# A hybrid encoder layer in float32: weights of the gates and of two forget-attention groups split ahead and kept in DRAM, dq projections two blocks to a bank, loads reckoned longer

## The chip, the cores and the metric

The kernel runs on one core of a Trainium2 chip. The metric is the device time of one launch in microseconds, the median of three runs. The core has five engines with queues of their own: TensorE (matmuls, PE in the profile, its weight loads PEld), VectorE (DVE), ScalarE (ACT), GpSimd (POOL) and SyncE (SP), which here issues the DMA transfers in order.

## The reference

One layer over 1024 positions of width 1024, in float32: a gated feed-forward, a mixer of two attention branches, and a second gated feed-forward, each behind a modulated RMS norm.

```python
x = x + 0.5 * mod[:, 0, 2][:, None, :] * swiglu(modulate(x, ...), ffn1_w1, ffn1_w3, ffn1_w2)
h = modulate(x, norm_g[l, 1], mod[:, 1, 0], mod[:, 1, 1])
z = h @ w_in      # fq, fk, fv, ff | dq, dk, dv, iq, ik, iw | ga, gb
ya = fox_attention(rms_norm(fq), rms_norm(fk), fv, cumsum(log_sigmoid(ff + bias)))
yb = dsa_attention(rope(rms_norm(dq)), rope(rms_norm(dk)), dv, iq, ik, iw, top_k=256)
x = x + g2 * ((sigmoid(ga) * (ya @ w_br_fox) + sigmoid(gb) * (yb @ w_br_dsa)) @ w_out)
x = x + 0.5 * mod[:, 2, 2][:, None, :] * swiglu(modulate(x, ...), ffn2_w1, ffn2_w3, ffn2_w2)
```

For this change the projection `h @ w_in` matters: the gates `ga`, `gb` (2 x 1024 columns), the four forget groups (two heads' fq, fk, fv each, 384 columns) and the two dq groups (256 columns).

## The kernel before

**Split numbers.** A float32 product is made of three matmuls (`mm3`, L435): every operand is split into a high part `hi`, its value rounded to the matmul's own format by a ScalarE copy, and a low part `lo = src - hi` by a subtraction on VectorE or GpSimd. `mm3` adds hi x hi, hi x lo and lo x hi in a PSUM bank.

**The stages.** (1) First feed-forward, 0 to 688 us: its three products by a Strassen-like scheme of seven products over 11 pairs of blocks. `up_all` walks through 130 steps of one product (12 matmuls each); per step `steps` may hold extra calls, and `extra` makes the conditioning vectors beside it. `Down` makes the second half. Weights are split as they are used, VectorE making the low parts. (2) Statistics of the norm (`stats`), a first small projection (`first`, `norm_apply`), and the first three weight pieces of the first forget group (`k.early`), 688 to 723 us. (3) Two forget groups beside the index scores, 723 to 850 us. (4) The top-k stage, 850 to 1050 us: VectorE and ScalarE find the 256th score of each row, 32 bits one after the other (`topk`: VectorE counts for three row blocks, ScalarE by signs for the other three), while TensorE works through forget groups 2 and 3, dq groups 0 and 1 and the 16 gate blocks of the first 512 positions. (5) Attention, 1050 to 1400 us, with the 16 gate blocks of the other 512 positions and the masks between. (6) The output product and the second feed-forward, to 2229 us.

**Loading a weight in the mixer.** `load_w` takes a raw tile from the ring `k.w`, loads into it, takes a pair `wh`, `wl`, copies on ScalarE and subtracts on GpSimd (`k.lo_eng`). Each ring has raw tiles and pairs: one raw and three pairs at first, three raws and five pairs in stages 3 and 4 (`r5`), two and two in the attention (`r2`). `Ahead` keeps three pieces loaded before their use (one in the attention). The gate weights `w_g` are 16 pieces of 128 x 1024, used once per half of the positions, so each is loaded and split twice; forget weights are 4 pieces of 128 x 768 per group, dq weights 4 of 128 x 512.

**PSUM.** In the top-k stage `pq` holds eight banks: two tiles `p2` of two banks each, and four tiles `pj` of one. A wide group (`group`, forget 2 and 3, dq 0 and 1) keeps eight accumulators, one per block of 128 positions, over four weight pieces; `chain8` deals it four halves of `p2` and four `pj`. In the last of the four rounds `done` copies each finished accumulator out on ScalarE (tile `qkv`). The gates accumulate in `pj`.

**The order.** The order of all engines is written out by a planner (`Plan`): each call becomes a task, and `flush` places the tasks by list scheduling with estimated lengths, in the rank of the program order plus `behind`; a task may take a new buffer only within a window of ranks (200 in the first feed-forward, 600 later). The queues then run in just that order, each instruction waiting for its operands. A transfer is reckoned by these lines:

```python
self.wire = max(self.wire, s + 1.3) + t.bytes / 345e3
end = self.wire + 0.7
```

A GpSimd task and a VectorE task that both use only SBUF are placed one after the other (`self.port`). `t512` takes half-kilocolumn buffers from a common ring, 52 of them in the first feed-forward.

## Time and profile before

| | |
|---|---|
| median of 3 runs | 2230.95 us (2229.25 to 2231.05) |
| the profiled execution | 2230.78 us, its span 2229.0 us |
| busy: TensorE, VectorE, ScalarE, GpSimd | 97%, 74%, 51%, 11% of the span |
| TensorE in the chain that ended last | 82% |
| moved by DMA | 315.88 MB, 142 GB/s on average |
| granted clock of TensorE, mean | 0.994 |

Busy time of TensorE counts overlapped matmuls, so the better measure of a stretch is its number of matmuls and its idle time. Nearly every instruction has one line (L425, where the planner issues), so tiles tell which operation a row is: `bs`, `b` are feed-forward accumulators, `p` and `pj` the halves of `p2` and the single banks of the mixer, `qkv` a projection copied out of PSUM, `ir` the relu of an index score, `tk...` the top-k, `pr` and `mn` the attention's scores and their row minimum, `pth`, `ptl` transposed weights of the attention split in two, `wr`, `wh`, `wl` a weight raw, high and low.

### The profile page before, as it was taken

Reading aid. Unit: us, or ns where it says so; the run is one execution under the profiler, and the core shown is the slowest. Engines: PE = TensorE matmul, PEld = TensorE weight load, DVE = VectorE, ACT = ScalarE, POOL = GpSimd, SP = SyncE. Lnnn points to the kernel's source line nnn. Section 1 sums busy time; section 2 is a strip of 40 time slices with the busy share of each in tenths; the row PEclk is TensorE's granted clock in tenths of the full one; section 3 lists DMA queues with packets and bytes.
Section 4 is the critical chain, followed back from the end, with each engine's and each line's share of the span. In section 5 each row is a group of like instructions: output and inputs, shape, how many; then the busy total and the mean of one; then the engine's idle time right before and its main releaser. Section 6 shows DMA issues by size and latency. Waiting matters only on the chain.

```text
span 2229.0 us, 31185 instructions
## 1 busy us (share of the span) xinstructions
PE 2166.7 (97%) x10700; PEld 1782.9 (80%) x10700; DVE 1638.6 (74%) x3095; ACT 1145.2 (51%) x2105; POOL 252.0 (11%) x225
## 2 busy tenths in 40 slices
PE   7999999999999999989999998999999999999999
PEld 5877788887889899977777777777778888888887
DVE  7968776688684698888887677498865755558665
ACT  5634433444464566787777677244443333334443
POOL 0000000000010222223445343000000000000000
PEclk9999999999999999999999999999999999999999
DMA  9245543695421323235232212596224443258520
GB/s 333 95 149 178 173 152 109 213 351 195 125 89 57 109 78 130 96 123 161 90 120 88 72 39 81 202 354 189 66 81 132 137 130 103 96 207 287 166 76 38
DMA packets 186267, 315.88 MB, mean 142 GB/s; under 512 B 27238, under 2 KB 51814, under 8 KB 186108
## 3 DMA queue, kind: packets, MB, share of 16 engines
q1 hardware_dynamic: 186108, 313.89, 42.4%
q8 instruction: 84, 1.38, 0.3%
q14 instruction: 75, 0.61, 0.1%
HBM read 237.53 MB, written 76.28 MB: 141 GB/s over the span
## 4 chain that ended last, share of the span: by engine, by line
PE 82%; DVE 8%; ACT 5%; DMA 3%; issue 2%; SPq 0%; POOL 0%; DVEq 0%; ACTq 0%; POOLq 0%
PE bs L425 34%; PE b L425 28%; PE py L425 7%; PE pj L425 6%; PE p L425 5%; PE pt L425 2%; DVE qkv L425 1%; ACT tks L425 1%; DVE xc L425 1%; DMA mraw<-in_ada_w 1%; DMA wr<-in_w_f 1%; ACT pth L425 1%; ACT pr L425 1%; ACT wh L425 1%; DVE wl L425 1%
## 5 line engine op out<-in xcount | busy, mean ns | idle before, releaser
L425 PE MATMUL bs<-h,wh 128*128 128x512 f32 x1728 | 543.0, 395 | 1.6 <-ACT bs L425 1.3
L425 ACT ACTIVATE wh<-wr 128x512 fp32r<-128x512 f32 (+2 forms) x366 | 246.5, 679 | 451.7 <-PE bs L425 208.3
L425 PEld LDWEIGHTS bs<-h,wh 128*128 128x128 f32 x1728 | 322.9, 188 | 81.9 <-ACT bs L425 5.7
L425 PE MATMUL b<-h,wh 128*128 128x512 f32 x1088 | 344.8, 397 | 5.7 <-ACT z L425 2.6
L425 PE MATMUL bs<-h,wl 128*128 128x512 f32 x864 | 338.7, 393 | 0.5 <-DVE wl L425 0.5
L425 DVE TENSOR_TENSOR wl<-wr,wh 128x512 fp32r<-128x512 f32 x308 | 205.4, 686 | 123.5 <-ACT wh L425 116.6
L425 PEld LDWEIGHTS b<-h,wh 128*128 128x128 f32 x1088 | 205.0, 189 | 55.5 <-ACT z L425 3.5
L425 PE MATMUL b<-h,wl 128*128 128x512 f32 x544 | 214.7, 395 | 0.1
L425 PEld LDWEIGHTS bs<-h,wl 128*128 128x128 f32 x864 | 162.2, 188 | 39.2 <-DVE wl L425 0.9
L425 ACT ACTIVATE wh<-a 128x512 fp32r<-128x512 f32 x132 | 83.3, 631 | 174.4 <-PE b L425 93.0
L425 POOL TENSOR_TENSOR wl<-wr,wh 128x1024 fp32r<-128x1024 f32 (+2 forms) x58 | 123.8, 2137 | 328.6 <-ACT wh L425 323.3
L425 DVE TENSOR_TENSOR wl<-a,wh 128x512 fp32r<-128x512 f32 x132 | 91.3, 692 | 88.1 <-ACT wh L425 83.5
L425 PE MATMUL b<-wh 128*128 128x512 f32 x352 | 137.2, 390 | 0.7 <-ACT mrow L425 0.7
L425 PE MATMUL b<-wh,wl 128*128 128x512 f32 x352 | 137.0, 389 | 0.0
L425 PE MATMUL b<-wl,wh 128*128 128x512 f32 x352 | 137.0, 389 | 0.0
L425 PE MATMUL pj<-wh,h 128*128 128x384 f32 (+1 forms) x512 | 125.8, 324 | 0.3 <-ACT wh L425 0.2
L425 PEld LDWEIGHTS b<-h,wl 128*128 128x128 f32 x544 | 102.8, 189 | 25.1 <-DVE wl L425 0.7
L425 DVE TENSOR_TENSOR z<-bs,z 128x512 f32<-128x512 f32 x116 | 79.3, 687 | 58.7 <-PE bs L425 36.8
L425 POOL TENSOR_SCALAR pr<-pr,mn 128x128 f32<-128x128 f32 (+7 forms) x128 | 100.0, 801 | 134.7 <-DVE mn L425 127.5
L425 DVE TENSOR_TENSOR wl<-g,wh 128x512 fp32r<-128x512 f32 x154 | 106.5, 694 | 2.5 <-ACT wh L425 2.5
L425 ACT ACTIVATE pr<-pr,mn 128x256 f32<-128x256 f32 (+7 forms) x128 | 98.4, 770 | 18.0 <-DVE mn L425 17.7
L425 PE MATMUL bs<-wl,wh 128*128 128x512 f32 x264 | 103.1, 391 | 2.1 <-DVE wl L425 1.9
(322 smaller groups left out, 4405.2 us busy)
## 6 DMA issues: line engine op xcount, KB each, us to landing
d_g<-z SPq DMA_DIRECT2D x154, 256.0 KB, 2.1
g<-d_g SPq DMA_DIRECT2D x154, 256.0 KB, 4.7
mraw<-in_ada_w SPq DMA_DIRECT2D x144, 256.0 KB, 5.3
wr<-in_w13a SPq DMA_DIRECT2D x112, 256.0 KB, 5.3
wr<-in_w13b SPq DMA_DIRECT2D x88, 256.0 KB, 4.6
wr<-in_w_g SPq DMA_DIRECT2D x32, 512.0 KB, 4.2
a<-in_w2a SPq DMA_DIRECT2D x44, 256.0 KB, 5.1
a<-in_w2b SPq DMA_DIRECT2D x44, 256.0 KB, 5.3
```

The lines of the kernel that those rows point to most:

```text
L425: getattr(getattr(self.tc.nc, e), t.op)(*map(real, t.a), **{n: real(v) for n, v in t.kw.items()})
```

## The change

Sixteen gate weight pieces and the eight pieces of forget groups 1 and 2 are split once during the first feed-forward, 48 half pieces in all: load, ScalarE copy, GpSimd subtraction, and two stores into DRAM buffers `d_wg`, `d_wf`. Forty of the half pieces are spread over steps 30 to 124 of `up_all` (80 calls, a load and split or a pair of stores each), with a rank 200 behind; the last eight come after the statistics of the norm. `load_w` then loads both parts directly into `wh`, `wl`, for all 32 gate loads and the forget groups 1 and 2; forget groups 0 and 3, dq and the branch weights stay as they were. The pairs are dealt in program order (`in_turn`). A dq group's two neighbouring blocks of positions share a bank, in four halves of `p2`, and one copy takes both out. The planner reckons every transfer as landing 1 us later, in all stages.

```diff
+def chain4(two):
+    while True:
+        t = two()
+        yield t[:, 0:H]
+        yield t[:, H:T]
...
-                end = self.wire + 0.7
+                end = self.wire + 1.7
...
-        return tuple(p.tile([128, D], F32R, tag=t, name=t, bufs=n) for t in ("wh", "wl"))
+        return tuple(p.tile([128, D], F32R, tag=t, name=t, bufs=n, in_turn=True) for t in ("wh", "wl"))
 def load_w(k, src, n):
     nc = k.nc
+    if isinstance(src, tuple):
+        t = k.w.pair()
+        for part, d in zip(t, src):
+            nc.sync.dma_start(part[:, :n].bitcast(F32), d)
+        return t
...
-    ps = []
+    ps, m = [], H // n
     for i in range(4):
         hi, lo = next(src)
         for tk in range(8):
-            if i == 0:
+            if i == 0 and tk % m == 0:
                 ps.append(ptile())
...
-                mm3(k, ps[tk][:, :n], hh, hl, hi[:, cs], lo[:, cs], i + c == 0, i == 3 and c == 1)
-            if i == 3:
-                done(tk, ps[tk])
+                mm3(k, ps[tk // m][:, tk % m * n:tk % m * n + n], hh, hl, hi[:, cs], lo[:, cs], i + c == 0,
+                    i == 3 and c == 1, tk % m > 0)
+            if i == 3 and tk % m == m - 1:
+                done(tk, ps[tk // m])
...
-        k.nc.scalar.activation(t[tk // 4][:, tk % 4, :], ps[:, :n], AF.Copy)
+        m = H // n if wide else 1
+        k.nc.scalar.activation(t[tk // 4][:, tk % 4 - m + 1:tk % 4 + 1, :], ps[:, :m * n].rearrange("p (a b) -> p a b", a=m),
+                               AF.Copy)
...
+            def parts():
+                for src, dst in todo:
+                    n = dst[0].shape[1]
+                    m = n if n <= H else n // 2
+                    for c in range(0, n, m):
+                        nc.behind = 200
+                        t, hi, lo = (t512(k, dt, "gw")[:, :m] for dt in (F32, F32R, F32R))
+                        nc.sync.dma_start(t, src[:, c:c + m])
+                        nc.scalar.activation(hi, t, AF.Copy)
+                        nc.gpsimd.tensor_sub(lo, t, hi.bitcast(F32))
+                        nc.behind = 0
+                        yield
+                        nc.behind = 200
+                        for d, x in zip(dst, (hi, lo)):
+                            nc.sync.dma_start(d[:, c:c + m], x.bitcast(F32))
+                        nc.behind = 0
+                        yield
...
+            gw = parts()
+            steps = {2: [more], 4: [more], 6: [more]}
+            for n in range(80):
+                steps.setdefault(30 + 96 * n // 80, []).append(lambda: next(gw, None))
...
             first(0)
             stats(1)
+            for _ in gw:
+                pass
             rb = norm_spread(k, rms[1], bank)
...
-            g0 = chain(fox_group(k, fp, fp, w_f[0], 0, pj), fox_group(k, fp, fp, w_f[1], 1, pj))
+            g0 = chain(fox_group(k, fp, fp, w_f[0], 0, pj), fox_group(k, fp, fp, d_wf[1], 1, pj))
...
+            bank4 = chain4(p2)
...
-                       dq_group(k, fp, fp, tp, ws, 0, lambda: next(bank8), 0.8), islice(gt, 15),
-                       dq_group(k, fp, fp, tp, ws, 1, lambda: next(bank8), 0.6), gt)
+                       dq_group(k, fp, fp, tp, ws, 0, lambda: next(bank4), 0.8), islice(gt, 15),
+                       dq_group(k, fp, fp, tp, ws, 1, lambda: next(bank4), 0.6), gt)
```

## Rows read from the trace of the kernel before

**Rows 1.** The table of stretches, of seven stages: us from the span's start, then for each engine its busy time and (x) its instructions, the granted share of TensorE's clock, the DMA engines' share and GB/s.

```profile
190.00:460.00 270.00, 269.71 (x1161) 216.29 (x1160) 192.90 (x306) 103.74 (x180) 0.00 (x0) 1.00 0.55 182
...
688.00:706.00 18.00, 18.00 (x99) 17.02 (x98) 12.15 (x29) 12.49 (x20) 0.00 (x0) 1.00 0.11 43
706.00:735.00 29.00, 27.66 (x146) 26.32 (x145) 0.38 (x2) 7.52 (x12) 9.79 (x9) 1.00 0.47 155
735.00:850.00 115.00, 108.06 (x629) 103.36 (x628) 98.42 (x182) 66.95 (x114) 21.93 (x15) 1.00 0.24 81
850.00:1050.00 200.00, 191.50 (x1075) 170.12 (x1073) 165.68 (x494) 157.76 (x290) 58.67 (x30) 0.98 0.38 122
1050.00:1400.00 350.00, 333.93 (x2306) 266.87 (x2304) 268.43 (x594) 250.93 (x548) 149.41 (x155) 0.98 0.28 85
...
1620.00:2229.00 609.00, 603.46 (x2622) 490.64 (x2620) 384.61 (x604) 241.42 (x420) 0.00 (x0) 1.00 0.40 133
```

**Rows 2.** The waits of TensorE in 735 to 1050 us: who waited for whom, us in total, times, the longest.

```profile
PE p L425 <- ACT ir L425: 4.6, 4, 1.9
PE p L425 <- ACT qkv L425: 4.3, 5, 1.5
PE pj L425 <- ACT qkv L425: 3.5, 1, 3.5
```

**Rows 3.** The order of time around the ends of the two dq groups, TensorE and ScalarE: start, length (us), engine, operation, and in brackets the idle time before it and what ended it.

```profile
949.07 0.50 PE L425 MATMUL p<-wh,h 128*128 128x256 f32 x2 [1.05 <-ACT qkv L425]
...
951.05 0.51 PE L425 MATMUL p<-wh,h 128*128 128x256 f32 x2 [1.48 <-ACT qkv L425]
...
994.01 1.15 ACT L425 ACTIVATE tks<-tkl,tkca 128x1024 bf16<-128x1024 uint16 x1
...
995.14 0.39 ACT L425 ACTIVATE qkv<-pj 128x256 f32<-128x256 f32 x1
...
995.58 0.72 PE L425 MATMUL pj<-h,wh 128*128 128x512 f32 x2 [3.52 <-ACT qkv L425]
```

**Rows 4.** The table of stretches (columns as in rows 1) for the time right after three pauses of TensorE.

```profile
951.50:956.00 4.50, 4.50 (x14) 3.54 (x14) 3.85 (x11) 4.40 (x10) 1.30 (x1) 0.62 0.18 52
...
995.50:1000.00 4.50, 4.42 (x12) 3.53 (x13) 4.29 (x15) 4.50 (x11) 0.11 (x1) 0.62 0.23 94
...
1067.90:1071.30 3.40, 3.40 (x20) 2.74 (x16) 2.40 (x6) 0.70 (x2) 1.95 (x3) 0.50 0.02 5
```

**Rows 5.** The order of time at the end of the second wide forget group, ScalarE and TensorE.

```profile
899.81 0.49 ACT L425 ACTIVATE qkv<-p 128x384 f32<-128x384 f32 x1 [0.55 <-PE p L425]
...
900.35 0.44 PE L425 MATMUL p<-wl,h 128*128 128x384 f32 x1 [0.58 <-ACT qkv L425]
```

**Rows 6.** The groups of instructions by shape in 850 to 1050 us, ScalarE and GpSimd: count, busy us, mean ns of one, idle time before them.

```profile
L425 ACT ACTIVATE wh<-wr 128x1024 fp32r<-128x1024 f32 x16 | 16.9, 1054 | 10.9 <-issue 10.9
...
L425 ACT ACTIVATE wh<-wr 128x512 fp32r<-128x512 f32 x8 | 5.0, 630 | 4.0 <-issue 3.4 <-POOL wl L425 0.6
...
L425 POOL TENSOR_TENSOR wl<-wr,wh 128x1024 fp32r<-128x1024 f32 x16 | 38.5, 2404 | 95.0 <-ACT wh L425 95.0
L425 POOL TENSOR_TENSOR wl<-wr,wh 128x512 fp32r<-128x512 f32 x8 | 10.3, 1292 | 45.3 <-ACT wh L425 45.3
```

**Rows 7.** The order of time at two subtractions of GpSimd, with VectorE's instructions beside them and one of the same kind without, and two TensorE instructions behind the second.

```profile
944.80 1.29 POOL L425 TENSOR_TENSOR wl<-wr,wh 128x512 fp32r<-128x512 f32 x1 [4.58 <-ACT wh L425]
...
944.83 1.28 DVE L425 TENSOR_SCALAR tkca<-tkkhi 128x3 f32<-128x3 f32 x1
...
989.08 0.17 DVE L425 TENSOR_SCALAR tkca<-tkkey 128x3 f32<-128x3 f32 x1
...
1062.36 2.38 POOL L425 TENSOR_TENSOR wl<-wr,wh 128x1024 fp32r<-128x1024 f32 x1
...
1062.90 2.25 DVE L425 SCALAR_TENSOR_TENSOR tke<-tkg,tkn,tke 128x384 bf16<-128x384 f32 x1
...
1066.68 0.47 PE L425 MATMUL p<-qs 64*128 64x448 f32 x1 [1.30 <-DVE mn L425]
1067.56 2.33 PE L425 MATMUL p<-qs 64*128 64x448 f32 x11 [0.41 <-DVE mn L425]
```

**Rows 8.** The waits of TensorE in 1050 to 1400 us (columns as in rows 2).

```profile
PE py L425 <- DVE ptl L425: 4.3, 9, 1.3
PE p L425 <- DVE mn L425: 3.2, 5, 1.3
```

**Rows 9.** The waits of TensorE in 190 to 460 us, and the table of stretches (columns as in rows 1) for the end of the first half of the first feed-forward and what follows it.

```profile
PE bs L425 <- DVE z L425: 0.3, 1, 0.3
...
400.00:435.00 35.00, 35.00 (x152) 28.35 (x152) 26.77 (x42) 13.32 (x23) 0.00 (x0) 1.00 0.54 180
435.00:456.00 21.00, 21.00 (x91) 16.69 (x90) 11.01 (x18) 8.64 (x15) 0.00 (x0) 1.00 1.03 367
...
502.00:524.00 22.00, 22.00 (x99) 18.12 (x97) 14.23 (x24) 7.77 (x14) 0.00 (x0) 1.00 0.22 82
```

**Rows 10.** The order of time of SP's queue in 688 to 735 us, and the waits of TensorE in the same stretch.

```profile
706.41 13.18 SPq L425 DMA_DIRECT2D wr<-in_w_f  x3
...
PE pj L425 <- POOL wl L425: 1.1, 1, 1.1
```

**Rows 11.** The page's part on DMA issues: destination and source, queue, count, KB each, median us from issue to landing.

```profile
wr<-in_w13a SPq DMA_DIRECT2D x112, 256.0 KB, 5.3
```

More of the change, by code (lines that the diff above doesn't have):

```diff
@@ L1981, in layer @@
         k.lo_eng = nc.gpsimd
-        dram = lambda shape, nm: dp.tile(shape, F32, name=nm)
+        dram = lambda shape, nm, dt=F32: dp.tile(shape, dt, name=nm)
+        split_in = lambda n, m, nm: [tuple(dram([128, m], f"d_{nm}{i}{x}") for x in "hl") for i in range(n)]
+        d_wg = split_in(16, D, "wg")
+        d_wf = [split_in(4, 768, f"wf{i}") for i in range(4)]
+        d_wq = [split_in(4, 512, f"wq{i}") for i in range(2)]
+        todo = [(w[i], d[i]) for w, d in (((w_f[1], d_wf[1]), (w_f[2], d_wf[2]), (w_g, d_wg))) for i in range(len(d))]
         d_x = dram([8, 128, T], "d_x")
@@ L2136, in layer @@
             more()
-            rest = up_all(k, pairs, head, [], {2: [more], 4: [more], 6: [more]}, lambda: down.loads(down.LEAD), chain(consts(), rest),
+            gw = parts()
+            steps = {2: [more], 4: [more], 6: [more]}
+            for n in range(80):
+                steps.setdefault(30 + 96 * n // 80, []).append(lambda: next(gw, None))
+            rest = up_all(k, pairs, head, [], steps, lambda: down.loads(down.LEAD), chain(consts(), rest),
                           (nc.vector, nc.vector), True, lambda n: n % 2)
@@ L2148, in layer @@
                 steps.setdefault(divmod(q, PAIRS), []).append(more_mod)
+            for q in range(0, 0):
+                steps.setdefault(divmod(q, PAIRS), []).append(lambda: next(gw, None))
             down.run(steps)
@@ L2218, in layer @@
             parts = []
-            for i, (w, n) in enumerate(((w_f[2], 768), (w_f[3], 768), (w_q[0], 512), (w_q[1], 512))):
-                parts += [(w[j], n, r5) for j in range(4)] + [(w_g[b], D, r5) for b in range(3 * i, 3 * i + 3)]
-            ws = Ahead(k, parts + [(w_g[b], D, r5) for b in range(12, 16)] + [(w_g[b], D, r2) for b in range(2)], 3)
+            for i, (w, n) in enumerate(((d_wf[2], 768), (w_f[3], 768), (w_q[0], 512), (w_q[1], 512))):
+                parts += [(w[j], n, r5) for j in range(4)] + [(d_wg[b], D, r5) for b in range(3 * i, 3 * i + 3)]
+            ws = Ahead(k, parts + [(d_wg[b], D, r5) for b in range(12, 16)] + [(d_wg[b], D, r2) for b in range(2)], 3)
             nc.flush(k.hh[0] + k.hl[0] + k.hh[1] + k.hl[1] + [t for w in ws.q for t in w])
```

2 lines of the change are left out of this document (1 added, 1 removed).

## The prediction

> **What bounds the kernel now.** I read the table of stretches first [rows 1]. TensorE is the bound everywhere: in 190 to 460 us it runs 1161 matmuls in 270 us, 232.6 ns each, with 0.3 us of waiting in all [rows 1, 9]. The change takes no matmul away, so it can only give back waits, and these lie unevenly: the busy columns leave 0.3 us idle in 190 to 460, but 6.9 in 735 to 850, 8.5 in 850 to 1050 and 16.1 in 1050 to 1400 [rows 1]. The reader should see in the same rows that ScalarE is busy 157.8 of 200 us and VectorE 165.7 of 200 in the top-k stage (850 to 1050): there TensorE waits for others. The last feed-forward (1620 to 2229) has 5.5 us to give in 609.
>
> Then I read who ended the waits. In 735 to 1050 the largest are ScalarE's copies of projections out of PSUM (qkv, 4.3 + 3.5 us) and ScalarE's relu (ir, 4.6) [rows 2]. The order of time shows where three of the qkv waits stand: 1.05 us at 949.07 and 1.48 at 951.05, both at the first matmuls of the second dq group, which the order puts ahead of the gates, and 3.52 at 995.58, when gate matmuls want a `pj` bank after the second dq group [rows 3]. ScalarE is not idle then: it copies `pj` at 995.14 only after a top-k sign of 1.15 us that began at 994.01 [rows 3]. Each pause is followed by a stretch of 4.5 us with a mean granted clock of 0.62, that is, some of it at 1.2 GHz instead of 2.4 [rows 4]. Lost there: 4.5 x 0.38 = 1.7 us each.
>
> **The change part by part.**
>
> (a) **Two blocks per bank in the dq groups.** A dq group now fills four half tiles of `p2`, none of `pj`. After either dq group four `pj` banks are free, the gates start at once, and `p2` has three gate blocks' time to be emptied. This removes 1.05 + 1.48 + 3.52 = 6.05 us and the two clock falls, 3.4: 9.5 us. What is late next: a `p2` tile is two banks, and the trace shows TensorE stopping between the halves of one tile. ScalarE's copy of half one began at 899.81 and took 0.49, and TensorE went on with half two at 900.35, after 0.58 idle [rows 5]. The dq groups now have two such tiles each. A copy of 512 elements is near the 630 ns of a 128x512 copy [rows 6], so a stop is about 0.75 us, four of them 3.0. Bounds: no stop at all (9.5 gained), or all of ScalarE's lateness returns inside the group (nothing gained). The row nearest to it is 899.81, where ScalarE was on time, so I take 9.5 - 3.0 = **6.5 us gained**.
>
> (b) **Gate and forget-group weights come split.** Each of the 32 gate loads loses a ScalarE copy (1054 ns) and a GpSimd subtraction (2404 ns) [rows 6]. In the top-k stage that is 16 x 1.05 = 16.9 us of ScalarE and 38.5 of GpSimd, in the attention as much again. ScalarE's part is off TensorE's path but stands in front of the copies of (a): I count it there. GpSimd's part is worth something where it holds VectorE. The trace shows the pair: GpSimd subtracts from 944.80 for 1.29 us, and a VectorE operation of 128x3, elsewhere 0.17 us, takes 1.28; at 1062.36 GpSimd subtracts a gate weight for 2.38, VectorE's mask step takes 2.25, and TensorE then waits 1.30 us for the row minimum that VectorE makes next [rows 7]. That wait, the 0.4 behind it and the clock at 0.50 for 3.4 us (1.7) make 3.4 us in one place [rows 4, 7]. Waits for VectorE's minimum and its `ptl` come to 7.5 us in the attention [rows 8]. I take **3.0 us gained** there; bounds 7.5 gained, and 2 lost if the new order is worse by one such pause. In 735 to 850 GpSimd was busy 21.9 us, mostly with such subtractions, beside a VectorE at 98 of 115 [rows 1]; of the 4.6 us behind the relu I take **2.0 gained** (0 to 4.6).
> The loads themselves double: two transfers straight into `wh`, `wl`, and no raw buffer. A load can start only when TensorE has left the pair. In the top-k stage four of five pairs are in use or ahead, which gives some three weights' time, a gate block being 24 matmuls, 5.6 us; in the attention there are two pairs, but 16 blocks share 350 us. A landing takes about 5 us [rows 11]. The stage moves 122 GB/s where 367 is reached elsewhere [rows 1, 9]. I cost it at nothing; without that lead each gate would show some microseconds.
>
> (c) **Forty of 48 pieces in the first feed-forward.** Steps 30 to 124 of 130, 12 matmuls each: 94 x 2.79 = 262 us, about 190 to 456. Added: 40 loads, 80 stores on SP, 40 copies (at most 0.63 us: 25 us of ScalarE, busy 104 of 270) and 40 subtractions (at most 1.29: 52 us of GpSimd, idle there) [rows 1, 6]. Bytes: 16 x 0.59 + 24 x 0.79 = 28.3 MB, 108 GB/s on top of 182 [rows 1]. At 400 to 435 that fits (180 + 108 of 367). At 435 to 456 the queue is full already [rows 9], and 2.3 MB, 6 us, move on; the hole at 502 to 524 with its share of 0.22 takes them. Every store on SP waits for GpSimd, and the weight loads queue behind it; these are asked for nine steps, 25 us, before use. The pieces also take about 5 buffers of the common ring of 52, and results waiting for one hold PSUM banks. VectorE goes from 193 to 245 of 270 if every subtraction holds it. I take **1.0 lost** (0 to 5).
> The Trainium skill, page "SBUF — State Buffer", section "SBUF: two separate sides", says that GpSimd and a VectorE operation with two SBUF inputs or in a two-port fast mode take a shared port pair as an exclusive lock, and that the loser waits for the whole instruction. By that rule the subtractions are not hidden from VectorE in the stage that they move to, which speaks against this half of the change; the rows at 944.80 and 1062.36 agree with it [rows 7]. Read as a mean it leaves the sum as it is, read as a run of blocked results it is the fourth case below.
>
> (d) **The last eight pieces after the first feed-forward.** They stand between the statistics at about 688 us and the loads of the first fox weights, which begin at 706.41 [rows 10]. Added: 8 loads, 16 stores (24 x 0.262 = 6.3 MB, 17.1 us at 367 GB/s), 8 copies (5.0 us), 8 subtractions (10.3 us). ScalarE is busy 12.5 of 18 us there, GpSimd 0, the queue 0.11 [rows 1]: they nearly fit. But the first weights come through one raw buffer, one after the other, and TensorE already waits 1.1 us for the last subtraction [rows 10]; any delay of the chain counts in full. I take **1.5 lost**; bounds 0, and 17 if the pieces stand in front of the weights whole.
>
> (e) **Loads reckoned 1 us longer.** The planner took 1.3 + 0.76 + 0.7 = 2.8 us for 256 KB, now 3.8; the page shows 5.3 [rows 11]. It does nothing on the chip but move consumers behind other work, all over the kernel. Where TensorE hardly waits it has little to give. **0**, with 3 either way.
>
> Sum: -6.5 - 3.0 - 2.0 + 1.0 + 1.5 + 0 = -9.0. The profiled execution took 2230.78 us (span 2229.0 and 1.8 around it), 0.2 below the median 2230.95: 2230.95 - 9.0 = 2222.
>
> **The rivals.**
> Two: more comes back. All of (a), 9.5, the whole 7.5 in the attention, 4.6 in 735 to 850, against the same 2.5 lost: -19, 2212; half way, 2216. For it: ScalarE loses 17 us in a stage where its order decides. Against: most attention waits are TensorE, ScalarE and VectorE in turn, without GpSimd.
> Three: the wait moves into the group. ScalarE is late because its signs wait for VectorE; then TensorE waits for the copy between two halves instead of behind the group, and (a) gives nothing: -2.5, 2228.5. For it the stop at 900.35 [rows 5], against it the lighter ScalarE.
> Four: the port. VectorE is blocked 40 times by up to 1.29 us in the first feed-forward; if one block in four reached TensorE, 13 us instead of 1: +3, 2234. Against: weights are split several products ahead there, and the waits are 0.3 us.
> Five, slower: the last eight pieces hold up the first fox weights. If none of them is moved before 706 us, SP has 17.1 us of their transfers in front of the chain; TensorE stands after the small projections and pays a clock fall, 1.7, besides: 18.8 instead of 1.5 makes +8.3, 2239. It outweighs the gain from a delay of 8.8 us on.
>
> **How the numbers follow.** The forecast 0.45 (its own range 2217 to 2227), two 0.20, three 0.17, four 0.05, five 0.13. Range 2213 to 2236: it takes in most of two and the milder half of five. A measurement tells 0.2%, 4.5 us, from no change. Faster: 0.38 of the forecast, all of two, 0.02 of three: 0.60. Slower: 0.11 of five and 0.02 of four: 0.13. Same: 0.27.
>
> **What would show it.** (a): no qkv wait at the ends of the dq groups, no granted clock under 1 there, and short qkv stops inside them. (b): no 1024-wide subtraction, fewer waits for VectorE's minimum after 1050. (c): 190 to 460 still at 233 ns a matmul, with GpSimd near 50 us. (d): the time from the statistics to the first fox matmul; over 8 us more would prove me wrong. A first feed-forward that loses more than 5 us would, too.

## The result and the profile after

The changed kernel takes **2208.52 us** (median of 4 runs, 2207.41 to 2208.82), the kernel before 2230.67 in the same comparison: a ratio of 0.9901, 95% interval 0.9884 to 0.9918. The forecast was 2222.0 with a range from 2213 to 2236, so the direction was right and the size was not: 22 us came back, not 9, and the time lies 4.5 us below the range. The profiled execution took 2208.82 us (span 2207.1).

Where the 22 us lie is read from the order of time, by the first TensorE instruction of each kind: the first matmul of forget group 0, the first score of the attention, the last matmul into its accumulators `py`.

| span of the profile, us | before | predicted | after | difference |
|---|---|---|---|---|
| start to the first forget matmul | 723.2 | +2.5 | 725.5 | +2.3 |
| from there to the attention's first score | 314.9 | -8.5 | 301.3 | -13.6 |
| the attention | 364.4 | -3.0 | 354.0 | -10.4 |
| the rest | 826.5 | 0 | 826.3 | -0.2 |
| whole span | 2229.0 | -9.0 | 2207.1 | -21.9 |

The table of stretches of the changed kernel (columns as in rows 1), cut at the same places of the work as [rows 1], and one stretch of 6.8 us:

```profile
190.00:463.00 273.00, 271.85 (x1166) 217.28 (x1165) 208.39 (x302) 120.56 (x218) 51.30 (x38) 1.00 0.78 265
...
708.00:737.00 29.00, 26.04 (x127) 24.45 (x126) 2.07 (x2) 9.12 (x16) 15.65 (x14) 0.91 0.80 280
737.00:852.00 115.00, 114.42 (x667) 111.15 (x667) 90.59 (x201) 67.02 (x118) 3.62 (x7) 0.99 0.35 124
852.00:1030.00 178.00, 176.63 (x1021) 158.79 (x1020) 146.73 (x475) 136.52 (x254) 16.50 (x11) 1.00 0.49 160
1030.00:1380.00 350.00, 338.28 (x2349) 270.38 (x2348) 267.16 (x594) 240.61 (x538) 119.08 (x143) 1.00 0.38 117
...
732.00:738.80 6.80, 5.74 (x18) 5.22 (x18) 0.00 (x0) 0.77 (x1) 3.42 (x2) 0.50 0.88 327
```

Beside [rows 1]: GpSimd falls from 58.67 to 16.50 us in the top-k stage and from 149.41 to 119.08 in the attention; TensorE's idle time falls from 6.9 to 0.6 us in the index scores and from 8.5 to 1.4 in the top-k stage; and the granted clock, 0.98 in the last two stages before, is 1.00. The first feed-forward runs at 273 / 1166 = 234.1 ns a matmul instead of 232.6, with 51.3 us of GpSimd's subtractions beside it. One new loss stands at 732: 6.8 us at a clock of 0.50.

The waits of TensorE in the changed kernel, for 737 to 1027 us (the whole answer) and the two largest of 1027 to 1380 (who waited for whom: us, times, longest); they answer to [rows 2, 8]:

```profile
PE p L433 <- ACT qkv L433: 2.0, 3, 0.7
...
PE py L433 <- DVE ptl L433: 4.1, 10, 1.2
PE p L433 <- DVE mn L433: 2.6, 5, 0.9
```

The relu waits (4.6) are gone, and of the `qkv` waits (4.3 and 3.5) 2.0 are left, none of them behind a dq group. The order of time shows two of these three, each between the two halves of one `p2` tile; here is the second:

```profile
985.20 0.60 ACT L433 ACTIVATE qkv<-p 128x512 f32<-128x512 f32 x1 [0.18 <-PE p L433]
...
985.85 0.40 PE L433 MATMUL p<-wh,h 128*128 128x256 f32 x1 [0.69 <-ACT qkv L433]
```

VectorE has the same instructions for the top-k in both kernels, but they take less time. Its groups of 128x3 operations by shape, from 830 us on (count, busy us, mean ns), first the kernel before, then the changed one:

```profile
L425 DVE TENSOR_TENSOR tku<-tkcnt,tklim 128x3 uint32<-128x3 f32 x32 | 11.7, 365 | 0.8
L425 DVE TENSOR_TENSOR tkv<-tksgn,tklim 128x3 f32<-128x3 f32 x32 | 11.4, 355 | 23.4 <-ACT tks L425 23.2
L425 DVE SCALAR_TENSOR_TENSOR tkkey<-tku,tkkey 128x3 uint32<-128x3 uint32 x32 | 7.3, 227 | 1.0
L425 DVE SCALAR_TENSOR_TENSOR tkcand<-tkkey,tkm 128x3 uint32<-128x3 uint32 x31 | 6.8, 219 | 0.9
```

```profile
L433 DVE TENSOR_TENSOR tkv<-tksgn,tklim 128x3 f32<-128x3 f32 x32 | 7.8, 245 | 24.0 <-ACT tks L433 23.5
...
L433 DVE SCALAR_TENSOR_TENSOR tkkey<-tku,tkkey 128x3 uint32<-128x3 uint32 x32 | 5.1, 160 | 0.9
L433 DVE TENSOR_TENSOR tku<-tkcnt,tklim 128x3 uint32<-128x3 f32 x32 | 5.1, 159 | 0.7
L433 DVE SCALAR_TENSOR_TENSOR tkcand<-tkkey,tkm 128x3 uint32<-128x3 uint32 x31 | 5.0, 161 | 1.0
```

Three of the four groups now have the mean that they have undisturbed, 160 ns; in the kernel before they had up to 365. The four together go from 37.2 to 23.0 us. That is small beside 22 us of TensorE, but the top-k is a chain through VectorE and ScalarE, and its end moved: the last step, VectorE's second write of `thr`, stood at 1049.2 and now stands at 1027.8. Before, it came 11.1 us after the attention's first score, now 1.0. Where these 21.4 us lie is told by the operation that opens each of the 32 steps (shortest, median and longest in ns, first and last start in us; before, then changed):

```profile
L425 DVE TENSOR_SCALAR tkca<-tkkey x32: 163/169/170, 843.2 to 1042.1; 128x3 f32<-128x3 f32 x32
```

```profile
L433 DVE TENSOR_SCALAR tkca<-tkkey x32: 164/169/171, 832.0 to 1022.8; 128x3 f32<-128x3 f32 x32
```

The chain starts 11.2 us earlier, so more than half of the 21.4 was made ahead of it, beside the index scores. From its first step to its last it takes 190.8 us instead of 198.9 (8.1), and the steps behind take 5.0 instead of 7.1.

The clock is the other part. The kernel before runs at a granted clock of 0.50 at 951.9, 996.2, 1067.9 and 1368.3 (3.4 us each) and at 1050.8 (6.8 us); half of that, 10.2 us, is lost, 6.8 of it in the attention. The changed kernel loses 3.4 at 732 and nothing from there to the attention's end. The waits for `mn` and `ptl` in the attention, 7.5 us before [rows 8], are still 6.7.

### The profile page after: what moved, and what is told of

Its sections match the earlier page's. It is cut to its first block, busy times and chain, and to the rows that moved or that the text cites. A ratio compares the mean times of both kernels' runs of the same rounds, so it can differ in the third digit from the quotient of the medians.

```text
span 2207.1 us, 31581 instructions
## 1 busy us (share of the span) xinstructions
PE 2161.0 (98%) x10700; PEld 1779.2 (81%) x10700; DVE 1630.2 (74%) x3095; ACT 1133.1 (51%) x2105; POOL 224.6 (10%) x233
## 4 chain that ended last, share of the span: by engine, by line
PE 88%; DVE 5%; ACT 3%; DMA 2%; issue 1%; POOL 0%; SPq 0%; DVEq 0%; ACTq 0%; POOLq 0%
PE bs L433 34%; PE b L433 29%; PE pj L433 9%; PE p L433 7%; PE py L433 7%; PE pt L433 3%; DMA mraw<-in_ada_w 1%; DVE xc L433 1%; ACT pr L433 1%; ACT pth L433 1%; DVE xb L433 1%; DVE wl L433 0%; DVE ptl L433 0%; DMA wr<-in_wbr 0%; DVE z L433 0%
## 5 line engine op out<-in xcount | busy, mean ns | idle before, releaser
L433 ACT ACTIVATE wh<-wr 128x512 fp32r<-128x512 f32 (+1 forms) x326 | 204.8, 636 | 375.4 <-PE bs L433 184.5
L433 PE MATMUL pj<-wh,h 128*128 128x384 f32 x384 | 104.9, 343 | 1.9 <-ACT wh L433 1.9
L433 PE MATMUL bs<-wh,wl 128*128 128x512 f32 x264 | 102.3, 389 | 0.0
```

What stands on the lines that cost most here:

```text
L433: getattr(getattr(self.tc.nc, e), t.op)(*map(real, t.a), **{n: real(v) for n, v in t.kw.items()})
```

## The experiments

The theory after the result: **GpSimd's subtractions are the cost**, through VectorE, the top-k chain and ScalarE's queue, and what the split weights give back is that. Rivals: the banks of the dq groups (the prediction's largest term), ScalarE's lighter load, and the longer reckoning. One more can't be taken apart here: the planner also keeps VectorE and GpSimd apart in its own reckoning, so a kernel with other subtractions has another order too. Fifteen kernels, each timed against the kernel before on the same chip (which took 2230.1 to 2232.0 there). The table gives the median, and from the one profiled execution of each the stages as above, with the time of the last top-k step against the attention's first score. A stage is from one execution, so a column can be several us off where that execution lies off its median: 4.1 under it in e3, 4.0 above it in e12, 3.3 in e10, 3.1 in e14, 3.0 in e11.

| kernel | median us | ratio, 95% | to first forget matmul | to the attention | last top-k step | attention | rest |
|---|---|---|---|---|---|---|---|
| before | 2230.67 | | 723.2 | 314.9 | +11.1 | 364.4 | 826.5 |
| after | 2208.52 | 0.9901 (0.9884, 0.9918) | 725.5 | 301.3 | +1.0 | 354.0 | 826.3 |
| e1_reckon_only | 2220.39 | 0.9954 (0.9939, 0.9968) | 722.6 | 315.4 | +11.1 | 358.2 | 824.4 |
| e2_banks_only | 2234.38 | 1.0017 (1.0007, 1.0026) | 726.6 | 317.4 | +17.4 | 362.9 | 827.6 |
| e3_split_only | 2230.09 | 0.9995 (0.9984, 1.0007) | 742.9 | 300.3 | -2.6 | 356.3 | 824.8 |
| e4_split_unused | 2226.29 | 0.9977 (0.9967, 0.9987) | 725.5 | 319.0 | +11.8 | 357.8 | 823.7 |
| e5_no_banks | 2207.79 | 0.9901 (0.9886, 0.9916) | 724.6 | 298.9 | -2.6 | 356.0 | 826.1 |
| e6_no_reckon | 2228.42 | 0.9995 (0.9983, 1.0007) | 742.5 | 300.3 | +0.9 | 356.8 | 826.6 |
| e7_all_pool | 2259.62 | 1.0135 (1.0120, 1.0150) | 725.7 | 329.8 | +26.8 | 378.1 | 823.8 |
| e8_all_act | 2210.31 | 0.9913 (0.9899, 0.9928) | 724.3 | 306.8 | +4.5 | 352.4 | 824.7 |
| e9_att_raw | 2207.37 | 0.9888 (0.9873, 0.9903) | 724.2 | 298.9 | +4.6 | 356.8 | 824.7 |
| e10_topk_raw | 2219.09 | 0.9936 (0.9920, 0.9953) | 725.3 | 304.9 | +15.8 | 364.6 | 825.9 |
| e11_fox_raw | 2224.49 | 0.9965 (0.9952, 0.9978) | 727.1 | 318.5 | +7.0 | 355.3 | 824.9 |
| e12_reckon27 | 2212.30 | 0.9913 (0.9898, 0.9929) | 735.7 | 302.6 | +0.9 | 353.5 | 822.8 |
| e13_reckon_ff1 | 2210.61 | 0.9917 (0.9889, 0.9945) | 725.2 | 302.0 | -1.5 | 356.8 | 824.6 |
| e14_reckon_att | 2227.62 | 0.9989 (0.9977, 1.0001) | 727.1 | 317.2 | +11.1 | 359.7 | 825.0 |
| e15_nobanks_attraw | 2208.71 | 0.9903 (0.9878, 0.9928) | 724.1 | 299.3 | -1.2 | 355.7 | 825.3 |

### One part alone

**e1_reckon_only**: the kernel before with every landing reckoned 1 us later.

```diff
-                end = self.wire + 0.7
+                end = self.wire + 1.7
```

> The kernel before with transfers reckoned 1 us longer and nothing else. Theory one (the split weights free ScalarE and GpSimd, and the attention's pauses with their clock falls go with them): 2228 to 2233 us, the attention still about 365 us long with its falls of the granted clock. Theory two (the new order by later landings takes the pauses out of the attention): 2215 to 2222, the attention some 8 to 10 us shorter. Theory three (the bank change starts the attention in a better state): as theory one.

**e2_banks_only**: `chain4` and the halved banks of the dq groups on the kernel before; no weight is split ahead.

```diff
-                       dq_group(k, fp, fp, tp, ws, 0, lambda: next(bank8), 0.8), islice(gt, 15),
-                       dq_group(k, fp, fp, tp, ws, 1, lambda: next(bank8), 0.6), gt)
+                       dq_group(k, fp, fp, tp, ws, 0, lambda: next(bank4), 0.8), islice(gt, 15),
+                       dq_group(k, fp, fp, tp, ws, 1, lambda: next(bank4), 0.6), gt)
...
```

> The kernel before with the dq groups two blocks to a bank in four halves of p2 (and the weight pairs dealt in program order), without split weights and at the old reckoning. Theory one: 2221 to 2225 us, 6 to 9 us gained in the dq groups and the gate block behind them, the attention as before. Theory two: the same. Theory three: 2211 to 2216, with the attention's 10 us in it.

**e3_split_only**: the changed kernel with 0.7 reckoned and the dq groups in eight banks; only the weights come split.

```diff
-                end = self.wire + 1.7
+                end = self.wire + 0.7
...
-    ps, m = [], H // n
+    ps, m = [], 1
...
```

> The changed kernel with one block per bank again (dq on eight banks) and the old reckoning: only the split weights are left. Theory one: 2214 to 2220 us, some 4 us gained in the forget groups, 8 to 11 in the attention, 2 lost in the first feed-forward, and the waits at the ends of the dq groups back. Theory two and three: 2226 to 2231, the attention within 3 us of before.

The banks alone gave nothing and cost 4 us; none of the three theories for e2 (2211 to 2225) had that. The waits of TensorE in e2 from 735 to 1044 us, and one row of the order of time, inside the first dq group:

```profile
PE p L433 <- ACT qkv L433: 9.2, 6, 3.5
```

```profile
953.74 0.39 PE L433 MATMUL p<-wh,h 128*128 128x256 f32 x1 [3.47 <-ACT qkv L433]
```

Before, TensorE waited 4.3 + 3.5 us for `qkv` in this stretch [rows 2]; with the new banks alone it waits 9.2, 3.47 of it between two halves of a `p2` tile. The wait moved into the group, as the third rival had it: with other banks to write, TensorE still waited for a late ScalarE.

The split weights alone (e3) changed the median by nothing that can be told, but the table shows two large opposite effects: 14.6 us less up to the attention and 8.1 less in it, which is about the gain of the whole change (13.6 and 10.4), and 19.7 us more up to the first forget matmul. So its time fell into the range of theories two and three, but its attention is 8.1 us shorter and not within 3, and no theory had the 19.7. ScalarE's waits there, in 190 to 480 us, are the answer, for e3 and then for the changed kernel:

```profile
ACT gw L433 <- DMA gw<-in_w_g: 33.1, 16, 5.4
...
ACT gw L433 <- DMA gw<-in_w_f: 16.5, 12, 3.9
```

```profile
ACT gw L433 <- DMA gw<-in_w_f: 12.3, 8, 2.5
```

One of them in e3's order of time, ScalarE, VectorE and TensorE:

```profile
341.16 0.63 ACT L433 ACTIVATE gw<-gw 128x512 fp32r<-128x512 f32 x1 [5.39 <-DMA gw<-in_w_g]
341.70 0.62 ACT L433 ACTIVATE wh<-wr 128x512 fp32r<-128x512 f32 x1
...
342.35 1.37 DVE L433 TENSOR_TENSOR wl<-wr,wh 128x512 fp32r<-128x512 f32 x1 [4.43 <-ACT wh L433]
...
346.18 0.68 DVE L433 TENSOR_TENSOR z<-bs,z 128x512 f32<-128x512 f32 x1
...
346.91 1.22 PE L433 MATMUL bs<-h,wh 128*128 128x512 f32 x2 [3.25 <-DVE z L433]
```

The copy of a piece stands 5.39 us at the head of ScalarE's queue for a load that has not landed. Behind it stands a copy that the feed-forward needs, for which VectorE waits 4.43 us; VectorE's `z` comes late, and TensorE waits 3.25 us for it. In all, TensorE waits 10.3 us for VectorE's `z` in e3's 190 to 690 (six times, the longest 3.3); that wait does not stand in the changed kernel. In the changed kernel ScalarE's waits for `in_w_g` are 7.3 us (the groups by shape, 190 to 463). e6 below, which lacks the longer reckoning alone, has e3's waits again (26.2 for `in_w_g`, 18.7 for `in_w_f`). So the reckoning is what makes the pieces cheap. Between e6 and the changed kernel, 26 of the 40 copies stand later in ScalarE's order, by up to five other instructions.

The reckoning alone (e1), without any piece, gave 10 us by the median; of the 8.4 us by which its profile is shorter, 6.2 are in the attention. What of its order does that was not settled (e14).

### One part taken away

**e4_split_unused**: the pieces are split and stored, but every load takes the raw weight and splits it again, as before the change; banks and reckoning are the changed kernel's.

```diff
-            g0 = chain(fox_group(k, fp, fp, w_f[0], 0, pj), fox_group(k, fp, fp, d_wf[1], 1, pj))
+            g0 = chain(fox_group(k, fp, fp, w_f[0], 0, pj), fox_group(k, fp, fp, w_f[1], 1, pj))
...
-                parts += [(w[j], n, r5) for j in range(4)] + [(d_wg[b], D, r5) for b in range(3 * i, 3 * i + 3)]
+                parts += [(w[j], n, r5) for j in range(4)] + [(w_g[b], D, r5) for b in range(3 * i, 3 * i + 3)]
...
```

> The changed kernel, but the gates and forget groups 1 and 2 load their raw weights and split them as before: all 48 half pieces are made and stored, and none is read. Theory one: 2220 to 2227 us (bank gain of 7 to 8 less 2 to 3 of the pieces' price, the attention as before). Theory two: 2212 to 2217. Theory three: 2212 to 2217.

**e5_no_banks**: the changed kernel with the dq groups in eight banks.

```diff
-    ps, m = [], H // n
+    ps, m = [], 1
...
-                       dq_group(k, fp, fp, tp, ws, 0, lambda: next(bank4), 0.8), islice(gt, 15),
-                       dq_group(k, fp, fp, tp, ws, 1, lambda: next(bank4), 0.6), gt)
+                       dq_group(k, fp, fp, tp, ws, 0, lambda: next(bank8), 0.8), islice(gt, 15),
+                       dq_group(k, fp, fp, tp, ws, 1, lambda: next(bank8), 0.6), gt)
```

> The changed kernel with one block per bank again (dq on eight banks): split weights and the longer reckoning stay. Theory one, as the first four runs left it (the split weights give the mixer's whole gain, the waits at the ends of the dq groups among it): 2207 to 2212 us, and no long wait at the ends of the dq groups. Theory of the record (banks give 6.5 us): 2213 to 2219, with waits of 3 to 6 us there.

**e6_no_reckon**: the changed kernel with 0.7 reckoned.

```diff
-                end = self.wire + 1.7
+                end = self.wire + 0.7
```

> The changed kernel with the old reckoning of transfers: split weights and banks stay. If the reckoning pays by taking ScalarE's in-order waits for the pieces' loads out of the first feed-forward: 2222 to 2228 us, the first feed-forward 14 to 19 us longer than in the changed kernel, the mixer as short as there. If it pays in the mixer: the first feed-forward as in the changed kernel and the loss behind 723 us.

Reading the split weights is worth 17.8 us (e4 against after), the reckoning 19.9 (e6, with 17.0 of it before the first forget matmul), the banks nothing (e5: 0.7 faster without, and the intervals cover each other). e4's time fell into the range of its first theory by luck: that range counted 7 to 8 us for the banks. With what was measured it is e1's 2220.4 with 3.8 for the banks (e2) and 2.3 for the pieces, 2226.5. All of TensorE's waits of e5 from 735 to 1023 us:

```profile
PE p L433 <- ACT qkv L433: 1.5, 3, 0.6
PE pj L433 <- ACT qkv L433: 0.7, 1, 0.7
```

With the old banks, the 1.05, 1.48 and 3.52 us behind the dq groups [rows 3] are 0.7 in one place. They went with the split weights, which gave ScalarE and VectorE their time back. Both count: with ScalarE's copies back (e8 below) the `qkv` waits from 735 us to the attention are 4.6 and 0.8, with the raw weights of the top-k stage back (e10) 4.2.

### Which engine's half of the split counts

Two kernels with the same loads and bytes, so that only the engine differs: in both, a weight's raw form is loaded and one of its parts from DRAM, and the other part is made on the chip. **e7_all_pool** loads the high part and lets GpSimd subtract; **e8_all_act** loads the low part and lets ScalarE copy.

```diff
-        t = k.w.pair()
-        for part, d in zip(t, src):
-            nc.sync.dma_start(part[:, :n].bitcast(F32), d)
-        return t
+        raw = k.w.raw()
+        nc.sync.dma_start(raw[:, :n], src[0])
+        hi, lo = k.w.pair()
+        nc.sync.dma_start(hi[:, :n].bitcast(F32), src[1])
+        k.lo_eng.tensor_sub(lo[:, :n], raw[:, :n], hi[:, :n].bitcast(F32))
+        return hi, lo
...
```

(e8 has, in place of the last two steps before the return:)

```diff
+        nc.sync.dma_start(lo[:, :n].bitcast(F32), src[2])
+        nc.scalar.activation(hi[:, :n], raw[:, :n], AF.Copy)
```

> The changed kernel, but for all split weights the high part alone is loaded and the low part is subtracted by GpSimd from the raw weight, loaded too: the same bytes, ScalarE's copies still gone, GpSimd's subtractions back. If GpSimd is what held the mixer (it holds VectorE, VectorE holds ScalarE): 2222 to 2230 us. If ScalarE's copies were it: 2208 to 2214.

> The counterpart: the low part is loaded and the high part is copied by ScalarE from the raw weight: the same bytes, GpSimd's subtractions gone, ScalarE's copies back. If GpSimd is what held the mixer: 2208 to 2214 us. If ScalarE's copies were it: 2222 to 2230. If each counts for itself: both this and its counterpart 2214 to 2222.

With ScalarE's copies, nearly all of the gain stays (2210.3, 1.8 us above the changed kernel), so ScalarE's lighter load isn't what gave it. With GpSimd's subtractions it is lost more than twice over (2259.6, 51 us above), and that is more than they can account for: the kernel before has as many subtractions of weights (58, 123.8 us; e7 58, 124.6) and is 29 us faster. e7's range was 2222 to 2230. Its top-k starts at 859.6, 27.6 us after the changed kernel's, and ahead of that it has this stretch (columns as in rows 1):

```profile
780.00:800.50 20.50, 16.21 (x49) 11.60 (x49) 17.78 (x30) 15.64 (x27) 0.00 (x0) 0.50 0.00 1
```

GpSimd does nothing there. TensorE has 49 matmuls in 20.5 us, at half the clock, and no forget matmul until 798.16: the order has them elsewhere. How much of e7's loss is order and how much the hold was not separated, so the case against GpSimd rests on e8 and on e10 and e11 below, and e7 serves to show how a hold looks. In e7 two of the groups of VectorE's 128x3 operations (830 to 1080 us) are long again:

```profile
L433 DVE TENSOR_TENSOR tkv<-tksgn,tklim 128x3 f32<-128x3 f32 x32 | 12.7, 396 | 28.9 <-ACT tks L433 28.6
L433 DVE SCALAR_TENSOR_TENSOR tkcand<-tkkey,tkm 128x3 uint32<-128x3 uint32 x31 | 11.3, 364 | 1.0
```

The rows at the end of its top-k show how this reaches TensorE. The order of time, GpSimd, VectorE and TensorE:

```profile
1077.51 2.48 POOL L433 TENSOR_TENSOR vst<-nat,vst 128x512 fp32r<-128x512 f32 x2 [9.73 <-DVE tkkl L433]
1079.95 4.63 POOL L433 TENSOR_TENSOR wl<-wr,wh 128x1024 fp32r<-128x1024 f32 x2
...
1077.54 1.25 DVE L433 SCALAR_TENSOR_TENSOR tkku<-tkku,tkkl 128x3 uint32<-128x3 uint32 x1
1078.83 1.19 DVE L433 TENSOR_SCALAR tkm<-tkku 128x3 int32<-128x3 int32 x1
1080.05 2.26 DVE L433 TENSOR_SCALAR tkm<-tkm 128x3 uint32<-128x3 uint32 x1
1082.35 2.26 DVE L433 TENSOR_TENSOR thr<-tkku,tkm 128x3 uint32<-128x3 uint32 x1
...
1086.36 2.92 PE L433 MATMUL p<-qs 64*128 64x384 f32 x12 [9.13 <-DVE mn L433]
```

Four operations that take 0.16 us each undisturbed take 6.96 together, and each ends where one of GpSimd's four subtractions ends (two `vst` in 2.48 us, two `wl` in 4.63). Behind them in VectorE's queue stands the attention's first row minimum, `mn`, and TensorE waits 9.13 us for it. The granted clock of the 5 us after that wait (1086 to 1091) was 0.54. In the kernel before the same place stands at the start of the attention, with shorter waits (GpSimd, VectorE, TensorE):

```profile
1046.43 2.51 POOL L425 TENSOR_TENSOR vst<-nat,vst 128x512 fp32r<-128x512 f32 x2 [4.86 <-DMA f<-d_f]
...
1046.47 1.28 DVE L425 SCALAR_TENSOR_TENSOR tkku<-tkku,tkkl 128x3 uint32<-128x3 uint32 x1
1047.78 1.19 DVE L425 TENSOR_SCALAR tkm<-tkku 128x3 int32<-128x3 int32 x1
...
1051.09 2.92 PE L425 MATMUL p<-qs 64*128 64x384 f32 x12 [0.86 <-DVE mn L425]
```

and its table of stretches (columns as in rows 1) right behind:

```profile
1050.80:1057.60 6.80, 6.51 (x25) 5.21 (x26) 5.53 (x20) 6.09 (x18) 4.01 (x5) 0.50 0.78 244
```

At 0.50 of the clock, that is 1.2 GHz, 6.8 us do the work of 3.4. In the changed kernel the same four operations ran from 1027.21 to 1027.97, before GpSimd's first `vst` at 1034.92, and no such stretch follows. The `vst` subtractions are in both kernels and belong to no weight: a top-k that ends earlier misses them.

### Which weights count

**e9_att_raw**: the attention's 16 gate weights raw. **e10_topk_raw**: the top-k stage's 16 gate weights raw. **e11_fox_raw**: the eight weights of forget groups 1 and 2 raw. In each, all pieces are still made, and the rest is the changed kernel.

```diff
-        ws.parts, ws.n = [(d_wg[b], D, r2) for b in range(2, 16)] + [(wbr[b], D, r2) for b in range(2)], 1
+        ws.parts, ws.n = [(w_g[b], D, r2) for b in range(2, 16)] + [(wbr[b], D, r2) for b in range(2)], 1
...
```

(These lines are e9's; e10 and e11 put `w_g` and `w_f` for `d_wg` and `d_wf` in the same way.)

> The changed kernel, but the 16 gate weights of the attention are loaded raw and split there as before. If the attention's 10 us come from GpSimd's subtractions in the attention itself: 2216 to 2220 us. If they come from the state in which the attention begins (top-k done earlier) and from the order: 2208 to 2212.

> The changed kernel, but the 16 gate weights of the top-k stage are loaded raw and split there as before (those of the attention and the forget groups stay split). If GpSimd holding VectorE in the top-k stage is the main cost: 2217 to 2224 us, 8 to 11 lost between the first dq group and the end of the gates, and more if the attention starts worse for it. If the gain is the attention's own: 2209 to 2213.

> The changed kernel, but the weights of forget groups 1 and 2 are loaded raw and split there as before. If GpSimd beside the index scores, which are VectorE's, costs TensorE its relu waits: 2212 to 2216 us, lost between 725 and 857. If the planner's order can hide eight subtractions: 2207 to 2210.

The attention's own 16 subtractions cost nothing that can be told (2207.4). The same 16 in the top-k stage cost 10.6 us by the median, and their place is the surprise: of the 13.6 us that e10's profile is longer than the changed kernel's, 3.6 lie up to the attention, where they run, and 10.6 in the attention, where they don't (the other stages give 0.6 back). Of the 10.6, 6.8 are clock, in two stretches that the changed kernel doesn't have (columns as in rows 1):

```profile
1047.20:1054.00 6.80, 6.13 (x26) 4.97 (x27) 5.52 (x22) 4.00 (x15) 1.64 (x4) 0.50 0.72 229
1074.50:1081.30 6.80, 6.69 (x37) 6.47 (x38) 4.20 (x14) 2.73 (x9) 4.36 (x4) 0.50 0.63 224
```

This execution was the slowest of e10's four (mean clock 0.995, the others 0.997 and 0.998), so the others paid less of that. Its 32 top-k steps take 204.3 us (834.6 to 1038.9) instead of 190.8, and the top-k ends 15.8 us into the attention. Over all runs the two columns go together: where the last top-k step comes at most 7 us after the first score, the attention takes 352 to 357 us; where it comes 11 us or more after, 358 to 378. But the same 11.1 stands beside 358.2 (e1) and 364.4 (before), so the lateness is not all. That it is a cause is shown in place by the rows at 1046 and 1077, for the rest of the stage it is argued from the columns.

The eight forget weights cost 16 us by the median, above the range of 2212 to 2216, and nearly all before the attention (17.2 of 18.7 in its profile). Their place in the table of stretches (columns as in rows 1), for e11 and then the changed kernel:

```profile
760.00:800.00 40.00, 38.44 (x215) 35.62 (x214) 31.31 (x49) 30.69 (x56) 7.97 (x4) 0.91 0.13 41
800.00:840.00 40.00, 34.68 (x184) 32.68 (x183) 36.09 (x58) 26.51 (x43) 6.93 (x3) 0.91 0.10 40
```

```profile
765.00:805.00 40.00, 40.00 (x236) 38.74 (x235) 36.02 (x57) 34.24 (x59) 0.00 (x0) 1.00 0.33 119
805.00:845.00 40.00, 39.42 (x227) 38.15 (x226) 33.77 (x85) 17.40 (x29) 0.00 (x0) 1.00 0.58 205
```

Seven instructions of GpSimd, 14.9 us (none in the changed kernel), stand beside VectorE's index scores; TensorE is idle 6.9 us in the 80, where it was 0.6, and each 40 us has lost 9% of its clock, which is one stretch of 6.8 us at 0.50 (784.6 and 832.4): 3.4 us. The chain can be read off: VectorE's sums `s` of 128x512 take 1106 ns instead of 749, ScalarE's relu `ir` waits 10.3 us for `s` (723 to 873 us) instead of 2.2 (725 to 860), TensorE waits 6.8 us for `ir` instead of none, and the top-k starts at 849.4 instead of 832.0. The price of one weight is that of its place: nothing in the attention, 0.7 us (10.6 / 16) in the top-k stage, 2.0 (16 / 8) beside the index scores.

### The reckoning

**e12_reckon27**: 2.7 us reckoned instead of 1.7, in the changed kernel.

```diff
-                end = self.wire + 1.7
+                end = self.wire + 2.7
```

> The changed kernel with transfers reckoned yet 1 us longer (2.7 us after the wire instead of 1.7). If what matters is that the reckoning is no shorter than the landing (2.8 and 3.8 us for 256 KB against 4.4 to 5.3 measured): 2203 to 2208 us, the last in-order waits for loads gone. If 1.7 already hides them: 2207 to 2211. If a later reckoning only moves the order: anything within 5 us of 2208.5.

**e13_reckon_ff1**: 1.7 in the first feed-forward (where the planner's window is 200) and 0.7 from the mixer on, in the changed kernel.

```diff
-                end = self.wire + 1.7
+                end = self.wire + (1.7 if self.window == 200 else 0.7)
```

> The changed kernel with the longer reckoning in the first feed-forward only; from the mixer on loads are reckoned 1 us shorter, as before. Theory one, the reckoning works through the 40 pieces in the first feed-forward: the first feed-forward ends as in the changed kernel (Down's first matmul at about 467), the mixer takes 655 to 657 us as with or without the reckoning (after 655.3, without 657.1), total 2208 to 2211. Theory two, the reckoning is worth as much in the mixer's order, as on the kernel before, where it gave 10 us: about 2218.

**e14_reckon_att**: the kernel before with 1.7 from the attention on, 0.7 ahead of it.

```diff
+        self.land = 0.7
...
-                end = self.wire + 0.7
+                end = self.wire + self.land
...
+        nc.land = 1.7
         ws.parts, ws.n = [(w_g[b], D, r2) for b in range(2, 16)] + [(wbr[b], D, r2) for b in range(2)], 1
```

> The kernel before with the longer reckoning from the attention on, and nothing else. Up to the attention it must be the kernel before (its first score at 1038). Theory one, the 10 us of the reckoning alone are the order of the attention and of what stands behind it: 2222 to 2224, 6 us of it in the attention. Theory two, they come from another order of the top-k stage, which the attention then inherits: 2230.

e13 settles where the reckoning works in the changed kernel: with it in the first feed-forward alone, 17.8 of its 19.9 us are there (2228.42 - 2210.61). ScalarE's order of the copies there is the same in e13 and the changed kernel. More is not better: e12, with 2.7, is 3.8 us slower than the changed kernel by the medians, and in its profile, which lies 4.0 above its median, the first forget matmul comes 10 us later (735.7). What of its order does that stays open. For the kernel before it stays half open: e14 is 2.5 us faster by the median, with an interval that touches 1, where e1 gained 10. In its profile the part from the attention on is 4.7 + 1.5 = 6.2 us shorter than before's, which is most of e1's 8.3 there, while the part ahead, the same instructions in the same order, took 6.2 longer in that execution. Its two theories (2222 to 2224, and 2230) stay undecided.

### Both parts that bring nothing

**e15_nobanks_attraw**: e5 and e9 together.

```diff
-    ps, m = [], H // n
+    ps, m = [], 1
...
-        ws.parts, ws.n = [(d_wg[b], D, r2) for b in range(2, 16)] + [(wbr[b], D, r2) for b in range(2)], 1
+        ws.parts, ws.n = [(w_g[b], D, r2) for b in range(2, 16)] + [(wbr[b], D, r2) for b in range(2)], 1
...
```

> The changed kernel without the two blocks per bank, and with the attention's 16 gate weights raw again (ScalarE copy and GpSimd subtraction). Theory one, neither brings anything here: each alone gave 2207.8 and 2207.4, both together 2206 to 2209. Theory two, each is covered by the other: with both gone the attention, without its lighter GpSimd and with a later start, loses 5 us or more, 2213.

2208.7: the banks and the attention's split weights can both go without loss. The changed kernel, e5, e9 and e15 lie between 2207.4 and 2208.7 and can't be told apart; none is shown to beat the changed kernel.

## Why the prediction was right and wrong

**(a), the banks, -6.5, was wrong in its cause.** I read who ended TensorE's waits behind the dq groups and gave the gain to the banks that were waited for. The row of ScalarE's sign at 994.01 told that ScalarE was late; I put its lightening to this term and did not ask what made it late. e2 has the banks and none of the gain, e5 the gain without the banks. The third rival named the mechanism (ScalarE is late because its signs wait for VectorE, and the wait moves into the group) and e2 shows it; but it took ScalarE's lateness as given, and the other half of the change removed it. The term is worth 0 here, and what I had put into it came with (b).

**(b), the split weights, -3.0 and -2.0, was right in its mechanism and too small**, and this is the step that put the time outside the range. Split weights without the longer reckoning give -22.2 from the first forget matmul to the attention's end (e6: 14.6 + 7.6, a profile near its median; e3 the same to 0.5, in the fastest of its ten executions). Weight by weight, the 2.0 that I took for the eight forget weights measured 16 (e11); the 3.0 for the attention's sixteen measured nothing (e9); and the sixteen of the top-k stage, to which I gave no gain but what ScalarE's copies do for (a), measured 10.6 (e10). These are taken away one at a time and don't add: reading all of them is worth 17.8 (e4). I priced GpSimd's hold of VectorE only where a TensorE wait stands right behind a blocked operation, as at 1066.68 [rows 7]. Three prices were left out. Held operations delay a whole chain: beside the index scores they delay the relu and with it the start of the top-k (11.2 us), in the top-k its 32 steps (8.1). What that chain still has to do when the attention begins, the attention pays (e10: 10.6 of 13.6, in one execution). And pauses cost clock as well: five stretches at 0.50 went from behind the first forget matmul, 10.2 us, of which the prediction counted three, 5.1 [rows 4]; the one at 1051 alone cost 3.4. I looked for the attention's gain in its own 16 subtractions, where there was none (e9), and in its waits for `mn` and `ptl`, which went from 7.5 to 6.7 only. The second rival, more comes back, had the direction but the same omissions; whole (2212) it is still 3.5 above the result, and half way to it is 2217 and not 2216.
By the Trainium skill, page "SBUF — State Buffer", section "SBUF: two separate sides", the loser of the lock waits for the other engine's whole instruction; the rows at 1077.54 to 1082.35 agree to 0.1 us, in four operations of 0.16 us.

**(c) and (d), the added work, +2.5, were right up to the first forget matmul: +2.3**, and the fourth and fifth rivals, both slower, did not come. Shortly behind it, at 731.80, TensorE waits 1.90 us for the copy of a first forget weight where it waited 0.24, 1.6 more with the wait behind it (1.06 after 1.10), and the clock at 732 costs 3.4 in this execution; the profiles of e5, e9, e13 and e15 have no such fall there. (d) was low by up to these two. And (c) was right only with (e). Without the reckoning the pieces cost 19 us there (e3 +19.7, e6 +19.3), by a wait that I had not named for ScalarE: I had priced its 40 copies by their length (25 us in a free engine) and not by what stands behind a copy whose load is late.

**(e), the reckoning, 0 with 3 either way, was wrong**: worth 19.9 us in the changed kernel and 10 alone. "Where TensorE hardly waits it has little to give" held for the first feed-forward as it was before, not for the 40 loads that the change put there. The 10 us alone came mostly in the attention, where TensorE does wait; their cause stays open (e14).

**The sum.** Alone, the three parts gave -10.2 (e1), +3.8 (e2) and -0.5 (e3), about -7 together; the change gave -22.2. They don't add, because the reckoning takes away the price of the pieces: it is worth 10.2 alone and 22.3 with split weights (e3 to e5), and the split weights are worth 0.5 alone and 12.6 with the reckoning (e1 to e5). That the terms of (a) came back at all, through another cause, was luck.

## What to carry to other kernels

When a helper engine holds another one, price it not at the waits that stand right behind, but by the chain that the held engine serves: read how late that chain ends, and what the next stage pays for it. Work put on an idle engine's in-order queue costs its wait for data, not its length; a schedule made by estimates must reckon that landing long enough (and here 2.7 was no better than 1.7). And test a cause by taking it away alone: giving TensorE other banks only moved the wait that showed at the banks.

## What the runs showed of the hardware

- A VectorE operation of 128x3 elements, 0.16 us, takes as long as the GpSimd subtraction that it falls into: 1.19 to 1.28 us beside one of 128x512, 2.26 beside one of 128x1024. One with a single tensor input is held too (the `tkm` at 1078.83 and 1080.05).
- The same two pauses of TensorE had different sequels: after 1.90 and 1.06 us near 732 the changed kernel ran 6.8 us at a clock of 0.50, while e9, after 1.86 and 1.27 us at 730 to 732, kept 1.00 (724 to 744 us). A clock fall after a short pause is a risk, not a fixed price.
- The same instructions in the same order, up to the attention, took 1038.1 us in the profile of before and 1044.3 in that of e14. Two more stretches of 3.4 us at half the clock (545.3 and 787.7) are 3.4 of these 6.2.
